# A two-layer hybrid backbone: where four stages meet, the order of projections, the pools and the weight buffers are changed

## The chip, the cores and the metric

The kernel runs on one core of a Trainium2 chip. A core has five engines with their own instruction streams: TensorE (PE) for matrix products and transposes, VectorE (DVE), ScalarE (ACT), GpSimd (POOL) and SyncE (SP); SP and POOL here mostly issue DMAs. [...] The metric is the device time of one execution in microseconds, the median of several runs.

## The reference

The network has two layers on 1024 latent tokens and 256 context tokens of width 1024, so 1280 rows, ten tiles of 128. Layer 0 runs neighbourhood attention (16 heads) beside a bidirectional mLSTM (4 heads of width 256), layer 1 a bidirectional HGRN2 (16 heads of 128, with forget gates from a sigmoid); each ends in an output projection from 2048 to 1024. Cut to what matters here:

```python
# layer 0
qa, ka, va, za, qb, kb, vb, ob, zb, g = split(h @ w_in)          # o and z gate the mLSTM heads
hb = mlstm_bidir(qb, kb, vb, g) * sigmoid(ob);  hb = rms(hb, h_norm)
y  = concat([oa * silu(za), hb * silu(zb)]) @ w_out              # 2048 x 1024
x  = x + gate * y
# layer 1
q, f_fwd, f_bwd, i, z = split(h @ w_in_c)
f  = lb + (1 - lb) * sigmoid(f_pre);   k = 1 - f;   decay = log f
o  = gla(q, k, i, decay fwd) + gla(reversed, decay bwd)          # 16 heads, context first, then latents
y  = (rms(o) * silu(z)) @ w_out_c;     x = x + gate * y          # latents only
```

## The kernel before

Every factor of a large product is split into a rounded part and a remainder (`split`, L70 to L72: a cast on ACT, a subtraction on DVE), and a product is three matmuls: high x high, low x high, high x low (`dense`, L117 to L119; `out_sum`, L729 to L731). TensorE therefore does 24 matmuls of 512 columns for an output tile over 1024 of the 2048 inputs.

Weights come slab by slab. `wblock` (L76) asks for a raw buffer of 128 x 512 (256 KB) from a pool, loads it by a DMA that SP issues (L97), and splits it. The raw buffers are few (tag "wraw" with 3, "woraw" with 4), so a load waits until the lo split of the slab that had the buffer before. The split slabs lie in a ring of 8 or in a block of their own. `out_y` (L710) loads the y of an output tile the same way, in two raw loads (L716, "wraw" with 3 buffers) and splits them to yh, yl, two tiles deep.

Memory is given out by pools that open and close like a stack, on a left and a right side. A new pool may take the place of one that was closed; the first instruction that writes there then waits for the last that used the old place. On each engine the instructions have a fixed order, which a planner in the framework sets at build time from costs and priorities; `filler()` gives the projections under it the lowest priority, so that they fill TensorE beside other work.

The stages at which the change works, with the lines of `build`:

- The filler projections of the mLSTM (L1067 to L1073): v, q, k of each head, and at last o and z of head 3. `proj_out` writes each result to memory (L272, POOL); `ml_load` (L370) reads v, q, k back, transposes, and forms the scores; `ml_rec` (L416) runs the recurrence (L448, L458) over ten tiles in both directions, and `ml_out` (L496) reads o and z (L502), normalizes (L507 to L510), transposes (L514), copies (L515) and writes y (L516).
- The first half of the inputs of layer 0's output, for the second 512 columns (L1080 to L1091), is run ahead into `oacc`, then the second half (L1094 to L1104, `out_tile`, L734 to L746), with the weights `w2` in a ring of 8. Beside it the weights of the other 512 columns (`w1`, `wo_half`, L705) are loaded, two slabs a tile, through "woraw" buffers of their own pool or of `yp`.
- The full tiles of the first 512 columns (L1121 to L1135), each followed by layer 1's norm and transposes (L226, L234, L236, and the split to hh, hl, L249 and L250). The first weights of layer 1 (`wf`) go through the raw buffers of pool `op0`.
- Layer 1 begins with `hg_proj` (L756): per direction the gates of the context and of two pieces of 512 latents, evicted by a sigmoid (L769, L770) into gFc and gF.
- At layer 1's end (L1148 to L1175) the output runs ahead in the same way over 8 tiles, then its second half, beside the loads of w1, then the other columns.

Of the kernel before, what the change touches and what calls it, by code (L numbers as in the profile page):

```python
# [9 lines left out]
F32 = mybir.dt.float32  # L10
F32R = mybir.dt.float32r
U8 = mybir.dt.uint8
AF = mybir.ActivationFunctionType
ALU = mybir.AluOpType
# [4 lines left out]
P = 128  # L19
D = 1024  # L20
KD = D // P
LAT = 1024
CTX = 256
T = LAT + CTX
NT = T // P
# [18 lines left out]
class Prog:  # L44
# [28 lines left out]

    def wblock(self, pool, tag, srcs, nk, n, rawp=None, rawb=3, rawt="wraw", later=None, ring=None):  # L76
        nc = self.nc
        step = max(1, 512 // n)
        ns = nk // step
        if ring:  # L80
            whole = None
            los, his = [], []
        else:
            whole = [self.t(pool, [P, ns, 512], F32R, tag + c, 1) for c in "lh"]
            los, his = [[w[:, i, :] for i in range(ns)] for w in whole]
        w = _W(his, los, step, n)

        def piece(i):
            if ring:
                los.append(self.t(pool, [P, 512], F32R, tag + "l", ring))  # L90
                his.append(self.t(pool, [P, 512], F32R, tag + "h", ring))
            raw = self.t(rawp or self.rawp, [P, 512], F32, rawt, rawb)
            r3 = raw.rearrange("p (k f) -> p k f", f=n)
            off = 0
            for s in srcs:
                c = s.shape[1]
                nc.sync.dma_start(  # L97
                    out=r3[:, :, off : off + c],
                    in_=s[i * step * P : (i + 1) * step * P].rearrange("(k p) f -> p k f", p=P),
                )  # L100
                off += c
            self.split(his[i], los[i], raw)

        for i in range(ns):
            if later is None:
                piece(i)
            else:
                later.append(lambda i=i: piece(i))
        return w
# [592 lines left out]
        nc.gpsimd.dma_start(out=self.yd[p2], in_=z)  # L702


    def wo_half(self, es, wsrc, b, side, raw=None, later=None):  # L705
        wp = es.enter_context(self.tc.tile_pool(name=self.nm("wo"), bufs=1, side=side))
        return self.wblock(wp, "wo", [wsrc[:, b * 512 : (b + 1) * 512]], 16, 512, raw or wp, 4 if raw else 8, "woraw", later)


    def out_y(self, tt, q, ysrc, yp, bufs):  # L710
        yh = self.t(yp, [P, 8, P], F32R, "yh", bufs)
        yl = self.t(yp, [P, 8, P], F32R, "yl", bufs)
        for k in range(0, 8, 4):
            yr = self.t(yp, [P, 512], F32, "wraw", 3).rearrange("p (j t) -> p j t", j=4)
            k0 = q * 8 + k
            self.nc.sync.dma_start(  # L716
                out=yr, in_=ysrc[k0 : k0 + 4, :, tt * P : (tt + 1) * P].rearrange("j p t -> p j t")
            )
            self.split(yh[:, k : k + 4, :], yl[:, k : k + 4, :], yr)
        return yh, yl  # L720


    def out_sum(self, ps, w, tt, qs, ysrc, yp, bufs, ys=None):
        mm = self.nc.tensor.matmul
        for q in qs:
            yh, yl = ys[q] if ys else self.out_y(tt, q, ysrc, yp, bufs)
            for k in range(8):
                kk = (q - qs[0]) * 8 + k
                mm(ps, lhsT=yh[:, k, :], rhs=w.h(kk), start=(kk == 0), stop=False)  # L729
                mm(ps, lhsT=yh[:, k, :], rhs=w.l(kk), start=False, stop=False)  # L730
                mm(ps, lhsT=yl[:, k, :], rhs=w.h(kk), start=False, stop=(kk == 8 * len(qs) - 1))  # L731


    def out_tile(self, w, b, tt, ysrc, xsrc, xt, yp, op, bufs, ys=None, part=None):  # L734
# [21 lines left out]
    def hg_proj(self, h, pool, w=None):  # L756
        nc, a = self.nc, self.a
        st = {}
        col = lambda i: a["wc"][:, i * 2048 + h * P : i * 2048 + (h + 1) * P]
        lb, olb = self.lb[:, 0, h : h + 1], self.lb[:, 1, h : h + 1]  # L760
        F = [self.t(pool, [P, 2, 512], F32, "gF", 2) for _ in range(2)]
        Fc = self.t(pool, [P, 2, CTX], F32, "gFc", 1)
        for d in range(2):
            w = w if w and d == 0 else self.wring([col(1 + d)], P)
            for t0, n in ((LAT, CTX), (512, 512), (0, 512)):
                ps = self.ps("mm", [P, n])
                self.proj_tr(ps, w, 0, t0, n)
                dst = Fc[:, d, :] if t0 == LAT else F[t0 // 512][:, d, :]
                nc.scalar.activation(dst, ps, AF.Sigmoid)  # L769
                nc.vector.tensor_scalar(out=dst, in0=dst, scalar1=olb, scalar2=lb, op0=ALU.mult, op1=ALU.add)  # L770
        q = {}
        w = self.wring([col(0)], P)
        for t0 in (512, 0):
            ps = self.ps("mm", [P, 512])
            self.proj_tr(ps, w, 0, t0, 512)
            q[t0 // 512] = self.t(pool, [P, 512], F32, "gq", 2)
            sg = self.t(pool, [P, 512], F32, "gsg", 1)
            nc.scalar.activation(sg, ps, AF.Sigmoid)
            nc.vector.tensor_tensor(out=q[t0 // 512], in0=sg, in1=ps, op=ALU.mult)
        return dict(F=F, Fc=Fc, q=q)  # L780

# [180 lines left out]
    def build(self):  # L962
        tc, nc, a = self.tc, self.nc, self.a
        dma = nc.sync.dma_start
        with ExitStack() as es:
# [19 lines left out]
            def load(name, shape, eng=nc.gpsimd):  # L985
# [12 lines left out]
                out=self.qkn, in0=qkn[:, 0:1], scalar1=qkn[:, 1:2], scalar2=0.125, op0=ALU.mult, op1=ALU.mult  # L998
# [25 lines left out]
            right = ExitStack()  # L1024
# [27 lines left out]
            with tc.tile_pool(name="na", bufs=2) as pool, self.pp.phase(tq=1, s=2, acc=1):  # L1052
# [12 lines left out]
                        z = self.na_z(p2 + 1, pool)  # L1065
                self.ml_ahead(*ahead[7])
            with self.filler():  # L1067
                for h in range(4):
                    for part in "vqk":
                        if (part, h) not in self.md:  # L1070
                            self.ml_ahead(part, h)
                for part in "oz":
                    self.ml_ahead(part, 3)  # L1073
            with tc.tile_pool(name="ml", bufs=2) as pool, self.pp.phase(s=2, acc=2):
                self.mask = self.t(pool, [P, 2, P], F32, "mmask", 1)
                dma(out=self.mask, in_=a["mmask"])
# [5 lines left out]

                wr = es.enter_context(ExitStack())
                yp = wr.enter_context(tc.tile_pool(name="oy", bufs=1, side="right"))
                acc = self.t(yp, [P, NT, 512], F32, "oacc", 1)
                rows = lambda q, b: a["woab"][q * D : (q + 1) * D, b * 512 : (b + 1) * 512]
                w = self.wblock(yp, "wo", [rows(0, 1)], 8, 512, yp, 4, "woraw", ring=8)
                for tt in range(NT):
                    ps = self.ps("mm", [P, 512])
                    self.out_sum(ps, w, tt, (0,), self.yd, yp, 2)  # L1090
                    nc.scalar.copy(acc[:, tt, :], ps)  # L1091
                w2 = self.wblock(yp, "wo", [rows(1, 1)], 8, 512, yp, 4, "woraw", ring=8)
            l0.close()
            l1 = es.enter_context(ExitStack())  # L1094
            lk = l1.enter_context(tc.tile_pool(name="hgk", bufs=1))
            with tc.tile_pool(name="op0", bufs=2) as op, ExitStack() as wl:
                self.gate_bc(0, op, 2, 1)
                later = []
                w1 = self.wo_half(wl, a["woab"], 0, "left", yp, later)
                for tt in [8, 9, 3, 4, 2, 5, 1, 6, 0, 7]:  # L1100
                    xt = self.t(op, [P, D], F32, "ox", 2)[:, 512:D]
                    self.out_tile(w2, 1, tt, self.yd, self.xin(tt), xt, yp, op, 2, part=acc[:, tt, :])
# [3 lines left out]
                    later = later[2:]  # L1106
# [10 lines left out]
                self.gate_bc(0, op, 2, 0)  # L1117
                wr.close()
                right = es.enter_context(ExitStack())
                self.open_h(right)  # L1120
                self.wp = right.enter_context(tc.tile_pool(name="w1", bufs=2, side="right"))  # L1121
                self.rawp = op
                self.slabs = 4
                wf = self.wring([a["wc"][:, 2048 : 2048 + P]], P)
                for tt in [8, 9, 4, 5, 6, 7, 0, 1, 2, 3]:
                    xt = self.t(op, [P, D], F32, "ox", 2)
                    dma(out=xt[:, 512:D], in_=self.x1[tt * P : (tt + 1) * P, 512:D])
# [7 lines left out]
            with l1:  # L1135
# [9 lines left out]
                    if h < 15:  # L1145
                        st = self.hg_proj(h + 1, pool)

                right.close()  # L1148
                yp = es.enter_context(tc.tile_pool(name="oy", bufs=1, side="right"))
                acc = self.t(yp, [P, 8, 512], F32, "oacc", 1)  # L1150
                rows = lambda q, b: a["woc"][q * D : (q + 1) * D, b * 512 : (b + 1) * 512]
                w = self.wblock(yp, "wo", [rows(0, 1)], 8, 512, yp, 4, "woraw", ring=8)
                for tt in range(8):
                    ps = self.ps("mm", [P, 512])
                    self.out_sum(ps, w, tt, (0,), self.yd2, yp, 2)
                    nc.scalar.copy(acc[:, tt, :], ps)
                w2 = self.wblock(yp, "wo", [rows(1, 1)], 8, 512, yp, 4, "woraw", ring=8)
            with tc.tile_pool(name="op1", bufs=2) as op, ExitStack() as wl:
                later = []
                w1 = self.wo_half(wl, a["woc"], 0, "left", yp, later)  # L1160
                for b, w in ((1, w2), (0, w1)):
                    self.gate_bc(1, op, 1, b)
                    for tt in range(8):
# [146 lines left out]
```

## Time and profile before

| | us |
|---|---|
| median of 3 runs | 3583.36 (3583.01 to 3583.39) |
| the profiled execution | 3583.22 |
| its span | 3581.4 |
| TensorE busy | 3516.8 (98%) |
| VectorE busy | 2216.1 (62%) |
| ScalarE busy | 1418.4 (40%) |
| mean granted TensorE clock | 0.992 |

A row of a timeline gives the start in microseconds, the busy time, the engine, line and operation, what is written from what, the number of instructions in the group, and in brackets the idle time of that engine before it and what ended it. PEld are weight loads of TensorE, SPq are DMAs that SP issues. A row of the windows gives a stretch, its length, the busy time of each engine, the granted clock, the busy share of the 16 DMA engines and the bandwidth. A row of the waits gives the waiting instruction, its releaser, the total, the number of times and the longest. L numbers are lines of the kernel before.

### The profile page before, as it was taken

The numbers are of one execution on the slowest core, as the hardware profiler recorded it, in microseconds if no ns is written. First come the engines' busy times: TensorE is split into PE (matmuls) and PEld (weight loads), VectorE is DVE, ScalarE is ACT, GpSimd is POOL, SyncE is SP. The second block draws the span as 40 slices with busy tenths as digits, with TensorE's granted clock in tenths as the row PEclk, the third lists the DMA queues.
The fourth block names the chain that finished last, engine by engine and source line by source line (L and its number), as shares of the span: only waits on it lengthen the run. The fifth ranks groups of instructions, "written<-read, shape, count | busy, mean of one in ns | idle before, by whom it ended". The sixth has DMA issues, their size and how long they took to land.

```text
span 3581.4 us, 65599 instructions
## 1 busy us (share of the span) xinstructions
PE 3516.8 (98%) x24954; PEld 3222.6 (90%) x24954; DVE 2216.1 (62%) x5976; ACT 1418.4 (40%) x3493; POOL 454.6 (13%) x752
## 2 busy tenths in 40 slices
PE   8999999999999999998999999999999999999998
PEld 5879999999999999997788999999999999999877
DVE  4646676666754765664666666666666666666653
ACT  5545555445533434433354333333333333333341
POOL 2222222122211212211010000000000000000000
PEclk9999999999999999999999999999999999999999
DMA  5532323232234434324752111111111111110263
GB/s 206 175 103 75 84 70 84 72 89 75 79 96 148 127 93 141 118 72 141 228 158 62 36 36 36 33 36 36 36 35 34 31 36 36 35 33 27 74 205 116
DMA packets 323051, 305.25 MB, mean 85 GB/s; under 512 B 29016, under 2 KB 280088, under 8 KB 322608
## 3 DMA queue, kind: packets, MB, share of 16 engines
q1 hardware_dynamic: 290704, 217.44, 20.9%
q0 software_dynamic: 32032, 83.61, 6.9%
q8 instruction: 197, 3.23, 0.4%
q14 instruction: 118, 0.97, 0.1%
HBM read 241.49 MB, written 59.30 MB: 84 GB/s over the span
## 4 chain that ended last, share of the span: by engine, by line
PE 88%; issue 5%; DMA 3%; DVE 1%; ACT 1%; POOL 1%; SPq 0%; POOLq 0%; DVEq 0%; ACTq 0%
PE mm L119 18%; PE mm L117 18%; PE mm L118 18%; PE s L880 6%; PE mm L729 2%; PE mm L731 2%; PE mm L730 2%; PE acc L674 2%; PE tr L654 2%; PE acc L458 2%; PE s L467 2%; DMA mld<-md 1%; PE acc L448 1%; PE acc L933 1%; PE s L909 1%
## 5 line engine op out<-in xcount | busy, mean ns | idle before, releaser
L119 PE MATMUL mm<-wh,hl 128*128 128x256 f32 x2560 | 748.9, 293 | 0.2 <-DVE hl L250 0.2
L117 PE MATMUL mm<-wh,hh 128*128 128x256 f32 x2560 | 746.5, 292 | 0.0
L118 PE MATMUL mm<-wl,hh 128*128 128x256 f32 x2560 | 745.4, 291 | 0.0
L119 PEld LDWEIGHTS mm<-wh,hl 128*128 128x128 f32 x2560 | 488.5, 191 | 11.1 <-issue 4.1
L117 PEld LDWEIGHTS mm<-wh,hh 128*128 128x128 f32 x2560 | 488.6, 191 | 7.7 <-issue 1.4
L118 PEld LDWEIGHTS mm<-wl,hh 128*128 128x128 f32 x2560 | 488.7, 191 | 7.1 <-issue 0.8
L117 PE MATMUL mm<-hh,wh 128*128 128x512 f32 (+1 forms) x1216 | 449.5, 370 | 5.9 <-ACT gFc L769 5.9
L118 PE MATMUL mm<-hl,wh 128*128 128x512 f32 (+1 forms) x1216 | 449.2, 369 | 0.0
L119 PE MATMUL mm<-hh,wl 128*128 128x512 f32 (+1 forms) x1216 | 448.7, 369 | 0.0
L119 PE MATMUL mm<-wzh,hl 128*128 128x256 f32 x1024 | 295.3, 288 | 0.0
L117 PE MATMUL mm<-wzh,hh 128*128 128x256 f32 x1024 | 294.2, 287 | 0.0
L118 PE MATMUL mm<-wzl,hh 128*128 128x256 f32 x1024 | 293.9, 287 | 0.0
L875 ACT COPY gksel<-gK 128x512 f32<-128x512 f32 x224 | 148.8, 664 | 317.0 <-PE s L880 159.9
L117 PEld LDWEIGHTS mm<-hh,wh 128*128 128x128 f32 x1216 | 230.3, 189 | 37.5 <-ACT gFc L769 6.2
L119 PEld LDWEIGHTS mm<-hh,wl 128*128 128x128 f32 x1216 | 230.3, 189 | 31.7
L118 PEld LDWEIGHTS mm<-hl,wh 128*128 128x128 f32 x1216 | 230.3, 189 | 30.8
L880 PE MATMUL s<-gQ,gksel 128*128 128x128 f32 x1792 | 254.9, 284 | 0.0
L729 PE MATMUL mm<-woh,yh 128*128 128x512 f32 x576 | 229.8, 400 | 5.6 <-DVE oacc L743 3.5
L880 PEld LDWEIGHTS s<-gQ,gksel 128*128 128x128 f32 x1792 | 231.4, 191 | 1.3
L731 PE MATMUL mm<-woh,yl 128*128 128x512 f32 x576 | 229.6, 399 | 0.8 <-DVE yl L72 0.8
L730 PE MATMUL mm<-wol,yh 128*128 128x512 f32 x576 | 229.3, 398 | 0.4 <-DVE wol L72 0.2
L71 ACT CAST wh<-wraw 128x512 fp32r<-128x512 f32 x240 | 147.2, 619 | 202.8 <-PE mm L118 126.2
(307 smaller groups left out, 7349.6 us busy)
## 6 DMA issues: line engine op xcount, KB each, us to landing
wraw<-yd SPq DMA_DIRECT2D x144, 256.0 KB
wraw<-in_wab_dram SPq DMA_DIRECT2D x112, 256.0 KB
md<-ev POOLq DMA_DIRECT2D x100, 256.0 KB, 2.7
wraw<-in_wc_dram SPq DMA_DIRECT2D x96, 256.0 KB
adar<-in_wada_dram POOLq DMA_DIRECT2D x32, 512.0 KB, 4.8
wraw<-in_wc_dram SPq DMA_DIRECT2D x128, 128.0 KB
adar<-in_wada_dram SPq DMA_DIRECT2D x16, 512.0 KB
wraw<-in_wab_dram SPq DMA_DIRECT2D x64, 128.0 KB
```

The source lines that it names most:

```text
L71: nc.scalar.copy(hi, x)
L117: mm(ps, lhsT=lh(k), rhs=rh(k), start=(k == 0), stop=False)
L118: mm(ps, lhsT=lh(k), rhs=rl(k), start=False, stop=False)
L119: mm(ps, lhsT=ll(k), rhs=rh(k), start=False, stop=(k == nk - 1))
L458: nc.tensor.matmul(num, lhsT=qc[:, j, :], rhs=C[d][:, j, :], start=False, stop=(j == 1))
L467: nc.tensor.matmul(u, lhsT=st["k"][c][:, j * P : (j + 1) * P], rhs=vw, start=True, stop=True)
L654: nc.tensor.transpose(pt[:nk, i, :], pr[:, o : o + nk], self.ident)
L729: mm(ps, lhsT=yh[:, k, :], rhs=w.h(kk), start=(kk == 0), stop=False)
L730: mm(ps, lhsT=yh[:, k, :], rhs=w.l(kk), start=False, stop=False)
L731: mm(ps, lhsT=yl[:, k, :], rhs=w.h(kk), start=False, stop=(kk == 8 * len(qs) - 1))
L875: nc.scalar.copy(ksel.rearrange("p (b s i) -> p b s i", s=2, i=h), pick(K))
L880: nc.tensor.matmul(pa[:, c, :].rearrange("p (b s i) -> p b s i", s=2, i=h), lhsT=ksel[:, c * P : (c + 1) * P], rhs=qp[:, c * nbc : (c + 1) ...
```

## The change

Four things are edited. The filler projects o and z of head 3 ahead of its v, q, k. The output that runs ahead becomes a function, `out_ahead`; in layer 0 its slab ring has 11 buffers in place of 8, in layer 1 it takes its raw buffers from the recurrence's pool (`rp`), and half of w2's slabs from the ring of the projections. `wo_half` takes a list of rings and uses the three "wraw" buffers that the y loads use; in layer 0 its last two slabs (`rest`) are loaded behind the second half, through the buffers of `op0`, into the projections' ring, whose pool now opens ahead of the pool of h. In `hg_proj` gFc and one gF lie in the open pool `hgk` (`self.fp`), and for the first head the context and second pieces of both directions are projected before the first pieces.

```diff
@@ -87,9 +88,11 @@
 
         def piece(i):
             if ring:
-                los.append(self.t(pool, [P, 512], F32R, tag + "l", ring))
-                his.append(self.t(pool, [P, 512], F32R, tag + "h", ring))
-            raw = self.t(rawp or self.rawp, [P, 512], F32, rawt, rawb)
+                pl, tg, nb = ring[i] if isinstance(ring, list) else (pool, tag, ring)
+                los.append(self.t(pl, [P, 512], F32R, tg + "l", nb))
+                his.append(self.t(pl, [P, 512], F32R, tg + "h", nb))
+            rp = rawp[0] if isinstance(rawp, list) else rawp or self.rawp
+            raw = self.t(rp, [P, 512], F32, rawt, rawb)
             r3 = raw.rearrange("p (k f) -> p k f", f=n)
             off = 0
             for s in srcs:
@@ -702,16 +705,15 @@
         nc.gpsimd.dma_start(out=self.yd[p2], in_=z)
 
 
-    def wo_half(self, es, wsrc, b, side, raw=None, later=None):
-        wp = es.enter_context(self.tc.tile_pool(name=self.nm("wo"), bufs=1, side=side))
-        return self.wblock(wp, "wo", [wsrc[:, b * 512 : (b + 1) * 512]], 16, 512, raw or wp, 4 if raw else 8, "woraw", later)
-
-
-    def out_y(self, tt, q, ysrc, yp, bufs):
+    def wo_half(self, wsrc, rings, raw=None, later=None):
+        return self.wblock(None, "wo", [wsrc[:, 0:512]], 16, 512, raw, 3, "wraw", later, ring=rings)
+    def out_y(self, tt, q, ysrc, yp, bufs, rp=None):
         yh = self.t(yp, [P, 8, P], F32R, "yh", bufs)
         yl = self.t(yp, [P, 8, P], F32R, "yl", bufs)
         for k in range(0, 8, 4):
-            yr = self.t(yp, [P, 512], F32, "wraw", 3).rearrange("p (j t) -> p j t", j=4)
+            yr = self.t(rp or yp, [P, 512], F32, "wraw", 3).rearrange("p (j t) -> p j t", j=4)
             k0 = q * 8 + k
             self.nc.sync.dma_start(
                 out=yr, in_=ysrc[k0 : k0 + 4, :, tt * P : (tt + 1) * P].rearrange("j p t -> p j t")
@@ -720,15 +722,30 @@
         return yh, yl
 
 
-    def out_sum(self, ps, w, tt, qs, ysrc, yp, bufs, ys=None):
+    def out_sum(self, ps, w, tt, qs, ysrc, yp, bufs, ys=None, rp=None):
         mm = self.nc.tensor.matmul
         for q in qs:
-            yh, yl = ys[q] if ys else self.out_y(tt, q, ysrc, yp, bufs)
+            yh, yl = ys[q] if ys else self.out_y(tt, q, ysrc, yp, bufs, rp)
             for k in range(8):
                 kk = (q - qs[0]) * 8 + k
                 mm(ps, lhsT=yh[:, k, :], rhs=w.h(kk), start=(kk == 0), stop=False)
                 mm(ps, lhsT=yh[:, k, :], rhs=w.l(kk), start=False, stop=False)
                 mm(ps, lhsT=yl[:, k, :], rhs=w.h(kk), start=False, stop=(kk == 8 * len(qs) - 1))
+    def out_ahead(self, wsrc, nt, ysrc, yp, ring, rp=None):
+        acc = self.t(yp, [P, nt, 512], F32, "oacc", 1)
+        rows = lambda q: [wsrc[q * D : (q + 1) * D, 512:D]]
+        raws = (rp or yp, 3 if rp else 4, "wraw" if rp else "woraw")
+        w = self.wblock(yp, "wo", rows(0), 8, 512, *raws, ring=ring)
+        for tt in range(nt):
+            ps = self.ps("mm", [P, 512])
+            self.out_sum(ps, w, tt, (0,), ysrc, yp, 2, rp=rp)
+            self.nc.scalar.copy(acc[:, tt, :], ps)
+        n = self.slabs if rp else 0
+        rings = [(self.wp, "w", n)] * n + [(yp, "wo", ring)] * (8 - n)
+        return acc, self.wblock(yp, "wo", rows(1), 8, 512, *raws, ring=rings)
 
 
     def out_tile(self, w, b, tt, ysrc, xsrc, xt, yp, op, bufs, ys=None, part=None):
@@ -758,16 +775,20 @@
         st = {}
         col = lambda i: a["wc"][:, i * 2048 + h * P : i * 2048 + (h + 1) * P]
         lb, olb = self.lb[:, 0, h : h + 1], self.lb[:, 1, h : h + 1]
-        F = [self.t(pool, [P, 2, 512], F32, "gF", 2) for _ in range(2)]
-        Fc = self.t(pool, [P, 2, CTX], F32, "gFc", 1)
-        for d in range(2):
-            w = w if w and d == 0 else self.wring([col(1 + d)], P)
-            for t0, n in ((LAT, CTX), (512, 512), (0, 512)):
-                ps = self.ps("mm", [P, n])
-                self.proj_tr(ps, w, 0, t0, n)
-                dst = Fc[:, d, :] if t0 == LAT else F[t0 // 512][:, d, :]
-                nc.scalar.activation(dst, ps, AF.Sigmoid)
-                nc.vector.tensor_scalar(out=dst, in0=dst, scalar1=olb, scalar2=lb, op0=ALU.mult, op1=ALU.add)
+        F = [self.t(p, [P, 2, 512], F32, "gF", 1) for p in (pool, self.fp)]
+        Fc = self.t(self.fp, [P, 2, CTX], F32, "gFc", 1)
+        todo = [(d, t0, n) for d in range(2) for t0, n in ((LAT, CTX), (512, 512), (0, 512))]
+        if w:
+            todo.sort(key=lambda x: x[1] == 0)
+        w = w or [None, None]
+        for d, t0, n in todo:
+            w[d] = w[d] or self.wring([col(1 + d)], P)
+            ps = self.ps("mm", [P, n])
+            self.proj_tr(ps, w[d], 0, t0, n)
+            dst = Fc[:, d, :] if t0 == LAT else F[t0 // 512][:, d, :]
+            nc.scalar.activation(dst, ps, AF.Sigmoid)
+            nc.vector.tensor_scalar(out=dst, in0=dst, scalar1=olb, scalar2=lb, op0=ALU.mult, op1=ALU.add)
         q = {}
         w = self.wring([col(0)], P)
         for t0 in (512, 0):
@@ -1065,12 +1086,11 @@
                         z = self.na_z(p2 + 1, pool)
                 self.ml_ahead(*ahead[7])
             with self.filler():
                 for h in range(4):
-                    for part in "vqk":
+                    for part in "vqk" if h < 3 else "ozvqk":
                         if (part, h) not in self.md:
                             self.ml_ahead(part, h)
-                for part in "oz":
-                    self.ml_ahead(part, 3)
             with tc.tile_pool(name="ml", bufs=2) as pool, self.pp.phase(s=2, acc=2):
                 self.mask = self.t(pool, [P, 2, P], F32, "mmask", 1)
                 dma(out=self.mask, in_=a["mmask"])
@@ -1082,21 +1102,19 @@
 
                 wr = es.enter_context(ExitStack())
                 yp = wr.enter_context(tc.tile_pool(name="oy", bufs=1, side="right"))
-                acc = self.t(yp, [P, NT, 512], F32, "oacc", 1)
-                rows = lambda q, b: a["woab"][q * D : (q + 1) * D, b * 512 : (b + 1) * 512]
-                w = self.wblock(yp, "wo", [rows(0, 1)], 8, 512, yp, 4, "woraw", ring=8)
-                for tt in range(NT):
-                    ps = self.ps("mm", [P, 512])
-                    self.out_sum(ps, w, tt, (0,), self.yd, yp, 2)
-                    nc.scalar.copy(acc[:, tt, :], ps)
-                w2 = self.wblock(yp, "wo", [rows(1, 1)], 8, 512, yp, 4, "woraw", ring=8)
+                acc, w2 = self.out_ahead(a["woab"], NT, self.yd, yp, 11)
             l0.close()
             l1 = es.enter_context(ExitStack())
-            lk = l1.enter_context(tc.tile_pool(name="hgk", bufs=1))
+            lk = self.fp = l1.enter_context(tc.tile_pool(name="hgk", bufs=1))
             with tc.tile_pool(name="op0", bufs=2) as op, ExitStack() as wl:
                 self.gate_bc(0, op, 2, 1)
                 later = []
-                w1 = self.wo_half(wl, a["woab"], 0, "left", yp, later)
+                wl1 = wl.enter_context(tc.tile_pool(name="wo1", bufs=1))
+                raws = [yp]
+                rings = [(wl1, "wo", 14)] * 14 + [None] * 2
+                w1 = self.wo_half(a["woab"], rings, raws, later)
+                rest = later[14:]
+                del later[14:]
                 for tt in [8, 9, 3, 4, 2, 5, 1, 6, 0, 7]:
                     xt = self.t(op, [P, D], F32, "ox", 2)[:, 512:D]
                     self.out_tile(w2, 1, tt, self.yd, self.xin(tt), xt, yp, op, 2, part=acc[:, tt, :])
@@ -1117,11 +1135,16 @@
                 self.gate_bc(0, op, 2, 0)
                 wr.close()
                 right = es.enter_context(ExitStack())
-                self.open_h(right)
                 self.wp = right.enter_context(tc.tile_pool(name="w1", bufs=2, side="right"))
+                rh = right.enter_context(ExitStack())
+                self.open_h(rh)
+                rings[14:] = [(self.wp, "w", 4)] * 2
                 self.rawp = op
+                raws[0] = op
+                for ld in rest:
+                    ld()
                 self.slabs = 4
-                wf = self.wring([a["wc"][:, 2048 : 2048 + P]], P)
+                wf = [self.wring([a["wc"][:, 2048 : 2048 + P]], P), None]
                 for tt in [8, 9, 4, 5, 6, 7, 0, 1, 2, 3]:
                     xt = self.t(op, [P, D], F32, "ox", 2)
                     dma(out=xt[:, 512:D], in_=self.x1[tt * P : (tt + 1) * P, 512:D])
@@ -1145,19 +1168,13 @@
                     if h < 15:
                         st = self.hg_proj(h + 1, pool)
 
-                right.close()
+                rh.close()
                 yp = es.enter_context(tc.tile_pool(name="oy", bufs=1, side="right"))
-                acc = self.t(yp, [P, 8, 512], F32, "oacc", 1)
-                rows = lambda q, b: a["woc"][q * D : (q + 1) * D, b * 512 : (b + 1) * 512]
-                w = self.wblock(yp, "wo", [rows(0, 1)], 8, 512, yp, 4, "woraw", ring=8)
-                for tt in range(8):
-                    ps = self.ps("mm", [P, 512])
-                    self.out_sum(ps, w, tt, (0,), self.yd2, yp, 2)
-                    nc.scalar.copy(acc[:, tt, :], ps)
-                w2 = self.wblock(yp, "wo", [rows(1, 1)], 8, 512, yp, 4, "woraw", ring=8)
+                acc, w2 = self.out_ahead(a["woc"], 8, self.yd2, yp, 8, self.rawp)
             with tc.tile_pool(name="op1", bufs=2) as op, ExitStack() as wl:
                 later = []
-                w1 = self.wo_half(wl, a["woc"], 0, "left", yp, later)
+                wl1 = wl.enter_context(tc.tile_pool(name="wo1", bufs=1))
+                w1 = self.wo_half(a["woc"], [(wl1, "wo", 16)] * 16, [yp], later)
                 for b, w in ((1, w2), (0, w1)):
                     self.gate_bc(1, op, 1, b)
                     for tt in range(8):
```

## The prediction

> **What bounds the kernel now.** I read the page's busy times first, then the waits of TensorE, then the windows and timelines of the stages that the diff touches.
>
> ```profile
> span 3581.4 us, 65599 instructions
> PE 3516.8 (98%) x24954; PEld 3222.6 (90%) x24954; DVE 2216.1 (62%) x5976; ACT 1418.4 (40%) x3493; POOL 454.6 (13%) x752
> ...
> PE tr L514 <- DVE mhs L510: 8.3, 2, 8.1
> ...
> PE mm L117 <- ACT gFc L769: 5.9, 1, 5.9
> PE mm L729 <- DVE oacc L743: 3.5, 2, 1.9
> ...
> PE mm L729 <- ACT woh L71: 2.1, 1, 2.1
> ```
>
> TensorE (PE) is busy 98% of the span. The arithmetic is unchanged, so only its idle time and its clock can move: 3581.4 - 3516.8 = 64.6 us of idle is the whole store, and the rows above (total, times, longest) hold the part of it at the edited seams. Beside idle time there is the clock after it:
>
> ```profile
> core 0: us, PE busy (x) PEld busy (x) DVE busy (x) ACT busy (x) POOL busy (x), PEclk, DMA share, GB/s
> 1632.83:1649.96 17.13, 7.40 (x20) 5.23 (x20) 7.12 (x17) 6.87 (x16) 2.17 (x3) 0.60 0.65 201
> 1721.55:1737.00 15.45, 11.12 (x39) 8.20 (x40) 10.30 (x17) 10.00 (x19) 0.00 (x0) 0.89 0.82 257
> 1737.69:1741.10 3.41, 3.41 (x10) 2.68 (x9) 3.41 (x7) 1.86 (x4) 0.19 (x1) 0.50 0.86 251
> 1737.00:1792.00 55.00, 55.00 (x237) 45.32 (x237) 36.96 (x59) 16.65 (x28) 5.46 (x10) 0.97 0.73 226
> 1911.78:1918.61 6.83, 4.89 (x12) 3.83 (x13) 2.49 (x5) 3.40 (x5) 0.00 (x0) 0.50 0.53 155
> 3444.30:3455.00 10.70, 8.39 (x29) 6.43 (x29) 9.98 (x17) 7.02 (x12) 0.54 (x1) 0.84 0.86 267
> 3455.00:3490.00 35.00, 35.00 (x155) 28.76 (x154) 24.52 (x39) 11.61 (x19) 3.78 (x7) 1.00 0.75 233
> ```
>
> After a gap the granted clock is 0.50 for some microseconds: 4.89 us of matmul at 0.50 behind the 5.92-us gap at 1907.81, so 4.89/2 = 2.4 us are lost again; 3.41 us behind the short gaps of 1721 to 1737, so 1.7 us each time. I add 2.4 us for a long gap, 1.7 for a short one.
>
> **The change part by part.** Plus is slower. What decides is how far ahead of TensorE the loads run. The raw buffers through which a load must pass come from pools, and where a new pool takes over the place of an old one, the first user waits for the old one's last user.
>
> *Head 3's o and z first.* In the old order the output gates o, z of head 3 are the last projection. Their write and read-back stand ahead of the output weights on SP:
>
> ```profile
> 1635.83 0.72 POOL L272 DMA_DIRECT2D md<-ev  x1 [6.37 <-issue]
> 1638.39 0.80 SPq L502 DMA_DIRECT2D mlz<-md  x2
> 1639.42 1.28 SPq L97 DMA_DIRECT2D woraw<-in_woab_dram  x3
> 1649.60 0.59 PE L729 MATMUL mm<-woh,yh 128*128 128x512 f32 x1
> ```
>
> The last projection ends at 1632.8, the first output matmul comes 17 us later. In between, 7.40 us of matmul, mostly at half clock, is worth some 4.4 us, so about 12.7 us are lost. In the changed order k is last; the same write (1635.83 to 1638.39) and read follow, now of k, and then transposes, scores and the first recurrence, so the first output matmul stands about 13.5 us behind the projection with some 5.5 us of work before it, half of that slow: about 9.7 lost. Gain 3, bounds -6 (the weights land while k makes its round trip) and +2 (everything else queues behind k). Now the whole recurrence of head 3 runs beside the ten ahead tiles instead of before them; its end moves from 1703 to the first tiles of the second half. That costs nothing by itself, but see the next part.
>
> *Eleven slabs, and the weights of the next half through y's buffers.* Eleven buffers let three slabs of the second half's weights be split early, and the first two tiles of that half then follow without a gap. That removes 2.1 + 1.6 + 0.6 us of gaps in 1721 to 1737 (15.45 - 11.12 = 4.3) and two slow stretches (3.4): gain 7.7. But the next weights (wo1) now use the three "wraw" buffers of the y loads, and their slabs are split into a pool that takes the place of head 3's working set. In the built order two or three wo1 loads fill these buffers during the ahead tiles, their splits wait for that place, and the y of the third tile waits for the splits. Before, the same release came at 1707.2, when nothing waited for it:
>
> ```profile
> 1681.95 0.22 DVE L481 TENSOR_SCALAR msm<-acc,thr 128x1 f32<-128x1 f32 x1 [1.43 <-PE acc L458]
> 1686.74 0.42 DVE L510 TENSOR_TENSOR mhs<-mhs,mlz 128x256 f32<-128x256 f32 x1
> 1702.24 0.27 PE L514 MATMUL tr<-ident,mhs 128*128 128x128 f32 x1
> 1703.29 0.37 ACT L515 ACTIVATE myt<-tr,hnb 128x128 f32<-128x128 f32 x1
> 1703.95 0.73 POOL L516 DMA_DIRECT2D yd<-myt  x1 [4.67 <-ACT myt L515]
> 1707.41 0.27 DVE L1108 MEMSET gzero<- 128x256 f32 x1 [3.70 <-PE mm L730]
> 1709.62 0.38 SPq L716 DMA_DIRECT2D wraw<-yd  x1
> 1716.35 0.62 ACT L71 CAST yh<-wraw 128x512 fp32r<-128x512 f32 x1 [2.96 <-DMA wraw<-yd]
> ```
>
> Counted from the last matmul of the second tile: head 3's last row of results needs 1681.95 to 1687.16 = 5.2 us after its last recurrence, the tile between covers 5.5, but DVE takes three such rows in order: 2 (0 to 4). Two transposes and copies: 1.5. Copy's end 1703.66 to the memset at 1707.41, which waits for the write: 3.75. Memset, a cast, two lo splits: 1.65. The y load: 3.4 (I take the nearest uncrowded load, 3.35 in the chain of waits below; 1709.62 to 1716.33 shows 6.7 in a crowd). Cast: 0.6. Sum 12.9, of which the four transposes are 0.6 work: 12.3 idle and 2.4 of clock. Against the 7.7 gained this is +7.0 (bounds -5, if the y load is in time, to +11).
>
> ```profile
> 1639.42 3.35 DMA woraw<-in_woab_dram
> ...
> 1726.99 5.15 DMA woraw<-in_woab_dram
> ```
>
> [...]
>
> *Three buffers for both.* In 1737 to 1792 237 matmuls took 55.00 us, 0.23 each. From then on each tile (24 matmuls, 5.5 us) draws two y and two wo1 loads through three buffers, which before had seven. One round is issue, landing 3.35, cast 0.62, lo 0.69 and two queues, about 5.1; four loads in three buffers take 4 x 5.1/3 = 6.8 us. Over eight tiles 27 loads need 27/3 x 5.1 = 46 us against 44 of matmul: +1.5 (0 to 6). In layer 1's second half the 29 remaining loads need 49.3 against 44, with some slack from the two y buffers: +3 (0 to 8). Before, both stretches (1737 to 1792, 3455 to 3490) had no PE gap.
>
> *The last two wo1 slabs and wf behind the second half.* These three loads go through op0's three "wraw" buffers and are split into pool w1, which takes the place of the old yh, yl, so the splits wait for the half's last matmul. The first full tile's y needs the same buffers. Before, wf alone stood so, and y had been fetched:
>
> ```profile
> 1781.72 0.69 DVE L743 TENSOR_TENSOR oacc<-mm,oacc 128x512 f32<-128x512 f32 x1 [2.40 <-PE mm L731]
> 1782.45 0.69 DVE L745 TENSOR_TENSOR og<-oacc,gbc 128x512 f32<-128x512 f32 x1
> 1783.25 1.15 ACT L71 CAST wh<-wraw 128x512 fp32r<-128x512 f32 x2 [10.17 <-DVE og L745]
> 1784.02 1.29 DVE L72 TENSOR_TENSOR wl<-wraw,wh 128x512 fp32r<-128x512 f32 x2
> ```
>
> The matmul ends at 1781.6; add, product, casts and the second lo end at 1785.3 (3.7 later). Only then y is issued: landing 3.4, cast 0.6, so TensorE idles 7.7 us with no other work in its order, and loses 2.4 of clock: +10.1 (7 to 12.5). I am surest of this term.
>
> *Forget gates in the open pool.* The gates no longer wait for op0's release, and TensorE runs both directions' first two pieces before the last. But the second direction's weights are loaded into pool hg, which lies where op0 was:
>
> ```profile
> 1907.41 0.46 ACT L234 ACTIVATE ntmp<-tr,ab 128x128 f32<-128x128 f32 x1 [4.30 <-PE tr L226]
> 1911.63 0.29 DVE L250 TENSOR_TENSOR hl<-ntmp,hh 128x128 fp32r<-128x128 f32 x1 [0.15 <-ACT hh L249]
> 1912.06 10.14 SPq L97 DMA_DIRECT2D wraw<-in_wc_dram  x9
> 1913.72 0.79 PE L117 MATMUL mm<-hh,wh 128*128 128x512 f32 x1 [5.92 <-ACT gFc L769]
> 1914.99 1.35 ACT L71 CAST wh<-wraw 128x512 fp32r<-128x512 f32 x2 [0.83 <-DMA wraw<-in_wc_dram]
> ```
>
> The old gap ended when the gate's copy got its place; the load is issued at 1912.06 and cast at 1914.99, 0.62 long. In the new order the next matmul needs this cast: 1915.6, plus 0.6 for a gate's copy that now stands ahead on ACT. The gap runs from 1907.8 to 1916.2, 8.4 in place of 5.9: +2.5 (0 to 4; -8.3 if the load is early).
>
> *Layer 1's end.* Before, four weight slabs and three y loads go out at once; the first output matmul comes 7.8 us after the last projection:
>
> ```profile
> 3372.21 0.28 PE L119 MATMUL mm<-wzh,hl 128*128 128x256 f32 x1
> 3372.53 1.76 SPq L97 DMA_DIRECT2D woraw<-in_woc_dram  x4
> 3380.30 0.80 PE L729 MATMUL mm<-woh,yh 128*128 128x512 f32 x1
> ```
>
> After, three slabs are there early, but the other five and the first y pass in order through three buffers: casts and lo's 2.0 to 3.2, a second round of 5.1, then y's landing and cast: 11.3 us. +3.5 (0 to 6). The second half's weights at 3444 follow through the same three buffers; by rounds of 5 us the last slabs come 2 to 5 us late where 2.3 + 1.7 are lost now: +1 (-4 to +4).
>
> Sum: -3 + 7.0 + 1.5 + 3 + 10.1 + 2.5 + 3.5 + 1 = +25.6. The profiled execution took 3583.22 (span 3581.4 and 1.8 around it), 0.14 below the median of 3583.36, so 3608.8 or 3609.
>
> **The rivals.** (1) The y loads at the first seam are early, so that only its gain remains: 14.7 less, 3594. For it: at 1709.62 y left right behind the release, with no lo ahead of it. Against: the built order puts wo1's loads first. (2) The three buffers bind: a landing midway between 3.35 and 5.15 makes a round of 6.0, so 54 and 58 us stand against 44 each, 24 in place of the 4.5 counted: 19.5 more, 3628. For it: a DMA share of 0.73 to 0.86 in these stretches; against: fewer loads in flight. (3) The other side: a place that is taken over holds no load back, at the third tile, at the half's end and at the gates; then 14.7 + 10.1 + 10.8 = 35.6 fall away, and it is 3573. It decides when these three waits together are under 3 us of their 35.6. Against it stands the row at 1783.25: wf's cast waited 10.17 us for exactly such a place.
>
> **How the numbers follow.** The forecast's case (3598 to 3622) gets 0.58, rival 1 (3587 to 3598) 0.2, rival 2 0.12, rival 3 0.06, and 0.04 is left within 0.2% (7.2 us, about what a measurement can tell from no change). Slower: 0.58 + 0.12 + 0.14 of rival 1 = 0.84; same 0.04 + 0.06; faster 0.06. The range 3587 to 3623 holds the forecast and rival 1 and leaves out the rest; the forecast's own is 3598 to 3622.
>
> **What would show it.** The waits of TensorE after: an L731 matmul (old L729) behind an ACT yh cast for 8 to 12 us at about 1720, again for 7 to 8 us at about 1780, an L120 matmul behind ACT wh for about 8 us at about 1915; no 8.1 behind mhs, and no gap at 1632 longer than 5. Slow stretches behind each. If the y casts follow their loads without a wait for a lo split, the first or second of these is wrong, and with both wrong so is the sign.

## The result, and the profile after

The changed kernel takes 3620.18 us (3618.58 to 3622.71, 4 runs) beside 3583.38 of the kernel before: 1.0099 times as long, 95% interval 1.0086 to 1.0111. The forecast was 3609 with a range of 3587 to 3623, so the result lies 3 us inside the upper end. The profiled execution has a span of 3616.8 us, 35.4 more than before; TensorE was idle for 90.2 us of it (3616.8 - 3526.6), 25.6 more, and the rest is in matmuls that ran slower. First the page's head, then the waits of TensorE (total, times, longest):

```profile
span 3616.8 us, 65601 instructions
PE 3526.6 (98%) x24954; PEld 3223.7 (89%) x24954; DVE 2221.3 (61%) x5976; ACT 1421.4 (39%) x3493; POOL 453.9 (13%) x752
```

```profile
PE mm L731 <- ACT yh L71: 21.9, 12, 12.7
PE mm L731 <- issue: 10.7, 2, 9.7
...
PE mm L120 <- ACT wh L71: 8.2, 1, 8.2
...
PE tr L390 <- DMA mkn<-md: 2.4, 1, 2.4
```

The 8.1 us behind mhs are gone, and so are the waits at the start of the second half. In their place stand three long waits, each of an output or gate matmul (L731 is the old L729, L120 the old L117) for the cast of a load that came late: 12.7 us at 1727, 9.7 at 1792 (put down to issue, with a y cast right ahead of it), 8.2 at 1931. The other eleven waits in the first row are short, 9.2 us together, and recur tile after tile.

The timeline around the first:

```profile
1726.75 0.37 ACT L518 ACTIVATE myt<-tr,hnb 128x128 f32<-128x128 f32 x1 [2.12 <-DMA yd<-myt]
1727.17 0.33 PE L517 MATMUL tr<-ident,mhs 128*128 128x128 f32 x1 [2.69 <-ACT myt L518]
1728.20 0.73 POOL L519 DMA_DIRECT2D yd<-myt  x1 [2.31 <-ACT myt L518]
1730.72 1.66 ACT L71 CAST woh<-wraw 128x512 fp32r<-128x512 f32 x3 [2.81 <-DMA yd<-myt]
1731.37 1.90 DVE L72 TENSOR_TENSOR wol<-wraw,woh 128x512 fp32r<-128x512 f32 x3 [0.40 <-ACT woh L71]
1733.06 0.98 SPq L718 DMA_DIRECT2D wraw<-yd  x2
1739.52 0.62 ACT L71 CAST yh<-wraw 128x512 fp32r<-128x512 f32 x1 [0.31 <-DMA wraw<-yd]
```

Head 3's last transpose ends at 1727.5; its result is written (1728.20), and only when the write has landed may the three wo1 loads, which sit in y's buffers, be split into the place that head 3 held (1730.72). Their lo splits free the buffers, y is issued at 1733.06 and cast at 1739.52.

The other two long gaps are of loads that had to wait for a place as well. At the half's end:

```profile
1794.07 1.66 ACT L71 CAST wh<-wraw 128x512 fp32r<-128x512 f32 x3 [10.27 <-DVE og L762]
1796.22 1.10 SPq L718 DMA_DIRECT2D wraw<-yd  x2
1801.44 1.37 ACT L71 CAST yh<-wraw 128x512 fp32r<-128x512 f32 x2 [0.19 <-DMA wraw<-yd]
```

The casts of the last two slabs and of wf wait until the last og of the half is computed; only behind their splits is y issued (1796.22), and it is cast at 1801.44. At the gates the second direction's weights are issued only behind the last work in op0's place (hl, 1935.48), at 1935.91, and cast at 1939.07:

```profile
1935.91 6.09 SPq L100 DMA_DIRECT2D wraw<-in_wc_dram  x6
1939.07 1.30 ACT L71 CAST wh<-wraw 128x512 fp32r<-128x512 f32 x2 [3.61 <-DMA wraw<-in_wc_dram]
```

The windows of the same execution, with the clock: the slow stretch at the gap of 1727, the eight tiles that follow, and the slow stretch at the gap of the half's end.

```profile
core 0: us, PE busy (x) PEld busy (x) DVE busy (x) ACT busy (x) POOL busy (x), PEclk, DMA share, GB/s
1729.02:1746.09 17.07, 5.90 (x14) 4.60 (x15) 7.81 (x15) 4.18 (x8) 1.12 (x2) 0.50 0.85 277
1740.19:1792.50 52.31, 48.87 (x192) 37.27 (x192) 31.54 (x49) 15.52 (x25) 3.80 (x7) 0.94 0.69 219
1797.28:1807.52 10.24, 5.36 (x13) 4.19 (x14) 2.77 (x4) 2.73 (x5) 0.00 (x0) 0.50 0.78 240
```

### The profile page after: what moved, and what is told of

Same layout as the page of the kernel before. It is cut to its first block, busy times and chain, and to the rows that moved or that the text cites. A ratio compares the mean times of both kernels' runs of the same rounds, so it can differ in the third digit from the quotient of the medians.

```text
span 3616.8 us, 65601 instructions
## 1 busy us (share of the span) xinstructions
PE 3526.6 (98%) x24954; PEld 3223.7 (89%) x24954; DVE 2221.3 (61%) x5976; ACT 1421.4 (39%) x3493; POOL 453.9 (13%) x752
## 3 DMA queue, kind: packets, MB, share of 16 engines
q8 instruction: 197, 3.23, 0.4%
## 4 chain that ended last, share of the span: by engine, by line
PE 87%; issue 5%; DMA 4%; DVE 1%; ACT 1%; POOL 1%; SPq 0%; POOLq 0%; DVEq 0%; ACTq 0%
PE mm L122 18%; PE mm L120 18%; PE mm L121 18%; PE s L901 6%; PE acc L677 2%; PE tr L657 2%; PE mm L731 2%; PE mm L733 2%; PE mm L732 2%; PE s L470 2%; PE acc L461 2%; DMA wraw<-yd 1%; PE acc L451 1%; DMA mld<-md 1%; PE acc L954 1%
## 5 line engine op out<-in xcount | busy, mean ns | idle before, releaser
L120 PE MATMUL mm<-wh,hh 128*128 128x256 f32 x2560 | 743.1, 290 | 0.0
L120 PEld LDWEIGHTS mm<-wh,hh 128*128 128x128 f32 x2560 | 488.6, 191 | 6.9 <-issue 1.4
L120 PE MATMUL mm<-hh,wh 128*128 128x512 f32 (+1 forms) x1216 | 449.4, 370 | 8.2 <-ACT wh L71 8.2
L120 PE MATMUL mm<-wzh,hh 128*128 128x256 f32 x1024 | 294.2, 287 | 0.0
L120 PEld LDWEIGHTS mm<-hh,wh 128*128 128x128 f32 x1216 | 230.7, 190 | 39.6 <-ACT wh L71 8.5
L72 DVE TENSOR_TENSOR wl<-wraw,wh 128x512 fp32r<-128x512 f32 x246 | 168.1, 689 | 134.4 <-ACT wh L71 132.2
L731 PE MATMUL mm<-woh,yh 128*128 128x512 f32 x524 | 213.8, 408 | 28.9 <-ACT yh L71 18.2
L732 PE MATMUL mm<-wol,yh 128*128 128x512 f32 x524 | 211.7, 404 | 0.0
```

What stands on the lines that cost most here:

```text
L72: nc.vector.tensor_tensor(out=lo, in0=x, in1=hi.bitcast(F32), op=ALU.subtract)
L120: mm(ps, lhsT=lh(k), rhs=rh(k), start=(k == 0), stop=False)
```

## The experiments

Each is compared with the kernel before on its own chip, where the median of that was between 3583.4 and 3586.8 us, so the ratios carry the comparison. A difference of ratios times 3583 us is given in us; each is good to some 5 us.

**Four repairs of the changed kernel, one at a time.** For the first, the fourth and the runs that combine them, `wblock` takes a pool, a tag and a number of buffers:

```diff
-            rp = rawp[0] if isinstance(rawp, list) else rawp or self.rawp
-            raw = self.t(rp, [P, 512], F32, rawt, rawb)
+            rp = rawp if isinstance(rawp, list) else [rawp or self.rawp, rawt, rawb]
+            raw = self.t(rp[0], [P, 512], F32, rp[1], rp[2])
```

*Own raw buffers for wo1 in layer 0:*

```diff
-                raws = [yp]
+                raws = [yp, "woraw", 4]
...
-                raws[0] = op
+                raws[:] = [op, "wraw", 3]
```

> The changed kernel, but the first 14 slabs of layer 0's next weights get the four woraw buffers again, so that y has its three for itself. Theory (the y load of the third tile queues behind weights whose place is not free): the 12.7-us wait behind yh at 1727 shrinks below 4, the four waits of 0.6 to 1.1 at 1754 to 1775 go, the slow stretch shortens; 15.4 + 3.0 + 6 less what stays: about 3598. Rival (it is head 3's late end: the splits of y stand behind the memset on VectorE that waits for the last y write): the gap stays at 8 or more, about 3610.

Measured 1.0069 (1.0054 to 1.0084). The wait at 1727 and the four short ones are gone, and yet only 11 us were won, because the next gap grew from 9.7 to 25.1. The chain of waits, and the timeline's row for the casts that wait for the half's place:

```profile
1769.62 0.23 PE mm L733
1769.85 25.07 issue
1794.92 0.77 PE mm L731
```

```profile
1764.38 19.34 SPq L756 DMA_DIRECT2D ox<-in_x_dram  x6
1783.57 0.69 DVE L762 TENSOR_TENSOR og<-oacc,gbc 128x512 f32<-128x512 f32 x1
1784.37 1.66 ACT L71 CAST wh<-wraw 128x512 fp32r<-128x512 f32 x3 [20.66 <-DVE og L762]
1789.28 2.95 SPq L718 DMA_DIRECT2D wraw<-yd  x3
```

The theory and the rival were each half right. y waited only by way of the shared buffers: with its own, no wait is left there. But head 3's late end holds more than y: the residual loads (ox, two buffers) lie in its place too, come only after it (the first at 1737.96), and take some 4 us a tile (the ox adds that wait for them, from 1767.33 to 1782.84, stand 3.66 to 4.08 us apart); TensorE runs ahead of them, and what needs the half's place (the last wo1 slabs, wf, and behind them y) waits for the last og at 1783.6, long after the last matmul at 1769.9. The step that moved head 3 and the step that shares buffers hide each other's cost.

*y of the first full tile ahead of the last slabs and wf:*

```diff
+                ys8 = {q: self.out_y(8, q, self.yd, op, 2) for q in (0, 1)}
                 for ld in rest:
                     ld()
...
-                    self.out_tile(w1, 0, tt, ..., op, op, 2)
+                    self.out_tile(w1, 0, tt, ..., op, op, 2, ys8 if tt == 8 else None)
```

> The changed kernel, but the y of the first full tile is asked for ahead of the last two slabs and wf; all else as it was. Theory (the three buffers were held by loads whose place was not free): the 9.7-us gap at 1792 and its 2.7 us of slow clock go, 3608. Rival (the splits that wait for the half's last matmul also hold the next tile's y or the last slabs, so the wait only moves): a gap of 4 or more within the first two full tiles, 3614 or later.

Measured 1.0072 (1.0055 to 1.0089), 10 us less than the changed kernel. From 1775 to 1925 the waits of TensorE hold one row:

```profile
PE mm L731 <- ACT yh L71: 0.2, 1, 0.2
```

The gap of 9.7 is gone, and nothing took its place (the mean granted clock is 0.991 for 0.990): the theory holds.

*The second direction's weights through op0's buffers:*

```diff
+                    if tt == 3:
+                        wf[1] = self.wring([a["wc"][:, 4096 : 4096 + P]], P)
```

> The changed kernel, but the second direction's first weights are loaded behind the last full tile's y through op0's buffers, into the projections' ring, and not through the pool that takes op0's place. Theory (the gap at 1931 is that pool's takeover plus a load): the 8.2-us wait behind wh goes with its 2.2 us of slow clock, 3610. Rival (the last tile's transposes and splits to hh, hl bound it anyway): 4 us or more stay at that place, 3615 or later.

Measured 1.0079 (1.0064 to 1.0094), 7 us less where 10 were expected. No wait of TensorE is left between 1900 and 1960, so the theory of the wait holds: from the last full tile's og to the first score matmul of layer 1 it is 52.2 us (1915.8 to 1968.0) in place of 62.7. The 3 us that are missing are within the scatter of such a difference. The mean granted clock of this execution was 0.988, that of the changed kernel's 0.990, though the two longest gaps had hardly changed (12.4 and 10.1 us for 12.7 and 9.7).

*Four raw buffers of its own for w1 in layer 1:*

```diff
-                w1 = self.wo_half(a["woc"], [(wl1, "wo", 16)] * 16, [yp], later)
+                w1 = self.wo_half(a["woc"], [(wl1, "wo", 16)] * 16, [yp, "woraw", 4], later)
```

> The changed kernel, but layer 1's w1 slabs get four raw buffers of their own again. Theory (four loads a tile through three buffers): the waits behind yh at the tiles of 3475 to 3515 (0.4 to 1.1 each, about 1.2 us a tile from start to start) go, 8 us less, 3612. Rival (the loads are bound by the DMA engines or their queue): the tiles stay at 6.6 us and the time at 3619.

Measured 1.0067 (1.0052 to 1.0082), 11 us less than the changed kernel. The waits of TensorE from 3465 to 3520, first of the changed kernel:

```profile
PE mm L731 <- ACT yh L71: 5.8, 7, 2.0
PE mm L731 <- issue: 1.1, 1, 1.1
PE mm L733 <- DVE yl L72: 0.4, 2, 0.2
```

then of this one:

```profile
PE mm L731 <- DVE oacc L760: 1.9, 2, 1.2
PE mm L733 <- DVE yl L72: 0.4, 1, 0.4
```

The waits behind yh are gone. From the last score matmul of the recurrence to TensorE's end layer 1 takes 207.5 us here, 214.0 in the changed kernel and 204.4 before: by these three executions 6.5 of the 9.6 lost there are the three buffers.

**Single edits on the kernel before.** *The ring alone:* `ring=8` becomes `ring=11` for w and w2 of layer 0.

> The kernel before with one edit, 11 slabs in place of 8 in the ring of layer 0's ahead tiles and w2. Theory (short gaps also cost slow clock): the gaps of 2.1, 1.6 and 0.6 us at 1721 to 1737 go, and the two slow stretches with them, 7.7 us faster, 3575.7. [...] Rival 2 (something behind, the residual loads or the next weights, takes the gain back): 3583.

Measured 0.9987 (0.9978 to 0.9997), 4.7 us. The slow stretches are gone, the gaps are not, as the waits from 1715 to 1770 show:

```profile
PE mm L729 <- DVE oacc L743: 3.0, 2, 2.1
PE mm L729 <- ACT yh L71: 0.6, 1, 0.6
PE mm L731 <- DVE yl L72: 0.4, 1, 0.4
```

That is 4.0 us of waits, 0.3 less than the 4.3 of before, only later: the loads of w2 and wo1 together still come late. So the theory that the gaps go is wrong. The span of this execution is 3.9 us shorter (3577.5 for 3581.4), and 0.3 of that are these waits, so I estimate that its gain is nearly all clock: before, two stretches of 3.41 us ran at 0.50 (from 1724.04 and 1737.69), here it was 1.00 from 1728 to 1745 (last section). The gaps alone (4.3) and the theory's number (7.7) both lie in the interval (1.1 to 7.9).

*o and z first alone:* the loop over the parts reads "ozvqk" for head 3, and nothing else changes.

> The kernel before with one edit, o and z of head 3 projected ahead of its v, q, k. Theory (the seam itself gains, but the late end of head 3 delays the second half's pools): the 8.1-us wait behind mhs goes, 5 us less at 1632; the residual loads of the second half start some 20 us later, and the wait of wf's cast behind og moves past the half's last matmul, with 0 to 10 us of TensorE waiting there: 3578 to 3588. Rival (head 3's late end costs nothing where y has its own buffers): 3578, no new wait over 2 us.

Measured 1.0006 (0.9996 to 1.0015): no change that can be told. The seam gains as in the changed kernel (8.1 and 1.5 become 0.6, 0.9, 2.2, 1.1 and twice 0.3), and TensorE ends the second half 7 us earlier than before (the last oacc add is at 1774.1 in place of 1781.7). The first full tiles behind it give most of that back. The waits from 1740 to 1810:

```profile
PE mm L729 <- ACT yh L71: 5.3, 4, 2.3
PE mm L731 <- DVE yl L72: 1.4, 1, 1.4
```

The two longest, 2.2 and 2.3 us at 1787 and 1797, are of full tiles. Before the first of them VectorE waited 3.1 us for a residual (ox, 1780.87), the yl split stood behind that (1781.48), and the next y was issued only when this split had freed its buffer (1782.19). So the late residual loads hold y even where y has raw buffers of its own, and the rival is out.

**All repairs together, and the first edit undone.** First the four repairs at once:

> The changed kernel with all four repairs at once: own raw buffers for the next weights in layer 0 and in layer 1, y of the first full tile ahead, the second direction's weights early. Theory (with y free, the half's tail is paced by the residual loads, which start when head 3 ends; the last two slabs then wait for the last og): the 25-us gap of the run with own raw buffers alone shrinks by the 11 us of the first full tile, to some 14 us, and stands in front of a matmul that needs the last slabs; gates and layer 1 gain 5 and 9: about 3587. Rival (it was y alone): no gap over 4 us at the half's end, 3571.

Measured 1.0003 (0.9994 to 1.0013), 3586.92 us where 3587 was expected. The four single repairs add up to 39 us and together they bring 34, the same within the scatter. The half's end still costs 11.4 us of waits in three pieces:

```profile
PE mm L731 <- ACT wh L71: 5.1, 1, 5.1
PE mm L731 <- ACT yh L71: 4.1, 1, 4.1
PE mm L732 <- DVE wl L72: 2.2, 1, 2.2
```

Then the same with o and z of head 3 last again:

> As the run with all four repairs, but o and z of head 3 are the last projection again, as in the kernel before. Theory (the late end of head 3 holds the second half's pools): no gap over 3 us at the half's end; the 8.1-us wait at 1632 is back; 7.7 us of the ring, 8.3 of the gates and 2 to 3 of layer 1's end are gained on the kernel before, about 3566. Rival (the residual loads or the own buffers bind by themselves): the gap at the half's end stays above 8, 3580 or later.

Measured 0.9973 (0.996 to 0.9985), by the medians 13.6 us less than with them first on the same chip (11 by the ratios), and faster than the kernel before. The first residual load is issued at 1709.31, with o and z first it was 1739.31. The gap at the half's end is gone; a 3.2-us wait at 1730 is left, behind w2's slabs.

Last, the first edit alone undone in the changed kernel:

> The changed kernel with its first edit alone undone: o and z of head 3 are the last projection again. Theory (the 12.7-us wait at 1727 needs both, buffers shared with y and a place that comes free only when head 3 ends): head 3 ends some 20 us before the half, the wait goes with 2.7 before it and 3 of slow clock, the 8.1 behind mhs comes back (5 net), the waits of 0.6 to 1.1 a tile and the 9.7 at the half's end stay: about 3607. Rival (the shared buffers alone): a wait of 8 or more behind yh stays at the second half's first tiles, and the time is 3625.

Measured 1.0066 (1.005 to 1.0081), 3609.67 us, 12 less than the changed kernel by the ratios. The waits from 1720 to 1780:

```profile
PE mm L731 <- ACT yh L71: 5.4, 4, 2.4
PE mm L733 <- DVE yl L72: 1.6, 2, 1.0
```

The 12.7 is gone though the buffers are shared as before: it needs both the shared buffers and a place that comes free only with head 3. The short waits stay, which need the sharing alone.

**A version that beats both.** The four repairs, o and z last, and six "woraw" buffers in layer 0:

```diff
-        raws = (rp or yp, 3 if rp else 4, "wraw" if rp else "woraw")
+        raws = (rp or yp, 3 if rp else 6, "wraw" if rp else "woraw")
...
-                raws = [yp, "woraw", 4]
+                raws = [yp, "woraw", 6]
```

> The run with four repairs and o, z last, with 6 woraw buffers in place of 4 in layer 0. Theory (w2's last slabs are late for want of raw buffers): the 3.2-us wait at 1730 shrinks below 1, 3570. Rival (the DMA engines are full there, a share near 0.8): more loads in flight land later, the wait stays and the time is 3573.

Measured 0.9957 (0.9944 to 0.9969), 3569.74 us. The wait at 1730 is gone; one of 0.57 at 1724, for a yl split, is the only one left between 1700 and 1800, though with four buffers the DMA share was 0.83 there (1730.5 to 1745). What is left at the seams is the old wait behind mhs and the start of layer 1's output:

```profile
PE tr L517 <- DVE mhs L513: 8.6, 2, 8.1
...
PE s L958 <- DVE gS L943: 3.1, 1, 3.1
PE mm L731 <- DVE oacc L760: 1.9, 2, 1.0
```

## Why the prediction was right, term by term

Sign and mechanisms held; the forecast sum of 25.6 came out some 10 us short (measured 35.4 between the traces, 36.8 between the medians). The measured terms are gaps of the changed kernel's trace with half of the matmul time in the slow stretches: at 0.50 14 matmuls of the half took 5.90 us (1740.19 to 1746.09), 0.42 each, where 237 before took 55.00, 0.23 each.

| term | forecast | measured |
|---|---|---|
| o and z of head 3 first | -3 | -5: 4.6 us of gaps for 9.6; 5.99 us of matmul at 0.50 for 6.39 |
| first seam, after the ring's gain | +14.7 - 7.7 | 2.69 + 12.69 + 5.90/2 = 18.3, less 7.7 |
| three buffers, layer 0 | +1.5 | 52.31 - 44 - 2.95 = +5.4 |
| last slabs and wf | +10.1 | 9.66 + 5.36/2 = 12.3 |
| forget gates | +2.5 | about +2 (8.2 for 5.9; 4.31 us of matmul at 0.50 for 4.89) |
| layer 1's end | +7.5 | +9.6, 6.5 of it the three buffers |
| sum | +25.6 | about +35 |

Two steps were mis-sized. One is the y load after a release, "I take the nearest uncrowded load, 3.35": at the first seam it took 6.46 from issue to cast (1733.06 to 1739.52), at the half's end 5.2 (1796.22 to 1801.44). The other steps of these two sums held within about a microsecond each. In the first this was in part luck: the 2 us counted for VectorE's rows were not there, and a copy of head 3 that waited 2.1 us for an earlier write (1726.75), which nobody had counted, stood in their place. The bound of 6.7 was in the prediction's own rows, and behind this release SP issued ten loads from 1730.80 to 1735.83, with a DMA share of 0.85 in the slow stretch, so the crowded row was the nearer one.

The other, larger one is "27 loads need 46 us against 44" and its like in layer 1. The formula of 6.8 us a tile is close: the waits end at 1754.7, 1761.9, 1768.9 and 1775.6, 6.7 to 7.2 us apart. But the count over all eight tiles lets a late load be made up for by an early one, and TensorE cannot catch up: four of the eight tiles paid 0.6 to 1.1 us of wait and some 0.5 behind it, 5.4 together where 1.5 was said; in layer 1 it is 6.5 where 3 was said. This is rival 2 at a good third of its size (7.4 of 19.5).

The gain of the ring, 7.7, was read as certain. The changed kernel did run the first two tiles of the half without a gap, but alone on the kernel before the ring gave 4.7, with the same gaps moved back; and 3.4 of the 7.7 were clock that one execution had lost, which the ring's execution did not lose behind a gap of the same length (last section). Rival 1 (y early) did not happen, rival 3 is ruled out by every repair: each wait went when its place or buffer came free earlier, and not before.

What the prediction did not see is a second wait that head 3's later end brings. It said "That costs nothing by itself, but see the next part", and the next part counts the place of head 3's working set, for wo1 alone. The residual loads wait for that place too and pace the half's tail. In the changed kernel the 12.7-us wait hides this; with all repairs it is the 11.4 us of waits above, and with o and z last, where the first residual load comes 30 us earlier, they are gone.

## What to carry to other kernels

When pools are stacked, ask of each early load not only whether a buffer is free but where its result goes: a load whose destination is not free yet holds its buffer, and everything that shares the buffer then waits for the old owner of that place. Share raw buffers only between loads that are freed at the same pace, and count loads per tile times the round trip over the buffers against the tile's matmul time. Price a load behind a release by the crowded row (6.46 us here, where the uncrowded one took 3.35), and where two edits meet, test them together and apart: here one of them hid a 25-us wait behind the other's 12.7.

## What the runs showed of the hardware

The length of a gap did not settle here whether the clock dropped. Before, 2.09 us at 1721.55 were soon followed by 3.41 us at 0.50:

```profile
1721.55:1723.64 2.09, 0.00 (x0) 0.00 (x0) 0.46 (x2) 0.67 (x2) 0.00 (x0) 1.00 0.91 304
1724.04:1727.45 3.41, 3.19 (x8) 2.37 (x8) 3.26 (x6) 3.41 (x8) 0.00 (x0) 0.50 0.73 220
```

With the ring of 11, 2.10 us at 1728.06 were followed by full clock:

```profile
1728.06:1730.16 2.10, 0.00 (x0) 0.03 (x1) 2.09 (x4) 2.05 (x4) 0.00 (x0) 1.00 0.45 136
1730.16:1745.00 14.84, 14.43 (x62) 11.62 (x63) 14.29 (x24) 8.43 (x15) 1.12 (x2) 1.00 0.88 268
```

With the four repairs and o, z last, 3.23 us at 1730.50 were too:

```profile
1730.50:1733.73 3.23, 0.03 (x1) 0.03 (x1) 1.44 (x3) 2.09 (x5) 0.00 (x0) 1.00 0.83 290
1733.73:1745.00 11.27, 11.27 (x49) 9.20 (x50) 11.27 (x20) 6.57 (x12) 1.12 (x2) 1.00 0.83 264
```

What decided it was not shown, so the 1.7 us that the prediction adds for a short gap is an estimate from the execution before, which the two others do not bear out.

Also, a short wait cost more than its gap. Behind the 1.14-us wait at 1760.8, at full clock (1.00 from 1759 to 1764), the first matmuls start 0.34, 0.39 and 0.33 us apart in place of 0.23:

```profile
1761.92 0.50 PE L731 MATMUL mm<-woh,yh 128*128 128x512 f32 x1 [1.14 <-ACT yh L71]
1762.26 0.40 PE L732 MATMUL mm<-wol,yh 128*128 128x512 f32 x1
1762.65 0.50 PE L733 MATMUL mm<-woh,yl 128*128 128x512 f32 x1
1762.98 0.40 PE L731 MATMUL mm<-woh,yh 128*128 128x512 f32 x1
```

From 1761.92 to 1762.98 is 1.06 for 0.69, some 0.4 us more. The matmul at 1762.26 waits for nothing that the trace names; ahead of the one at 1762.65 the weight load waited 0.43 us for yl.
